# Even mixer of a hybrid trunk: the depthwise convolution shared between VectorE and TensorE by channels and token parity, with the weight splits of that stage on VectorE

## The chip, the core and the metric

The kernel runs on one core of one Trainium2 chip. The metric is the device time of one execution in microseconds. The median of three runs of the kernel before is 970.71 us (969.78 to 971.41). TensorE is the matrix engine, VectorE (DVE), ScalarE (ACT) and GpSimd (POOL) are the three engines for elementwise work, SyncE (SP) issues the weight loads.

## The reference

The program is a trunk of two layers on 256 tokens of 1024 channels, all in float32. Each layer is a gated feed-forward, a token mixer and another feed-forward, each added to the residual. The mixer of the first layer, the even one, is the stage of this case:

```python
def even_mixer(h, w_in, w_out, conv_w, conv_b, ln_g, ln_b, q_g, k_g, sinks):
    proj = h @ w_in
    a_val, a_gate, q, k, v = jnp.split(proj, cuts, axis=-1)      # 512, 512, 512, 128, 128 columns
    u = a_val * jax.nn.sigmoid(a_gate)
    u = lax.conv_general_dilated(u, ...) + conv_b                # causal, per channel, 31 taps
    u = jax.nn.silu(layer_norm(u, ln_g, ln_b))                   # over the 512 channels
    q = rms_norm(q, q_g); k = rms_norm(k, k_g)                   # per head of 64
    o, _, _ = banded_attention(q, k, v, 127, sinks)              # 8 query heads, 2 key heads
    return jnp.concatenate([u, o], axis=-1) @ w_out
```

`h` is the residual after a root-mean-square norm with a gain per channel; the factor `1/rms` of a token is applied after the product.

## The kernel before, in words

Activations lie with tokens on partitions, in two halves `t` of 128 tokens and two halves `d` of 512 channels. A product needs them transposed as the stationary operand (four 128x128 blocks through `transposed`, L238), and streams the weights. Every float32 product is carried by three passes: both operands are split exactly into `hi` and `lo` (L308), and hi·hi, lo·hi and hi·lo are summed in PSUM.

**Weights.** A plan lists units of up to 128x2048. `take` keeps four of them in flight: SyncE loads a unit into a raw buffer, ScalarE copies it to `hi`, and the difference `lo` comes from VectorE in pieces of 1024 columns or, for the units named in `on_pool` (10 of the even mixer, 5 of the odd one), from GpSimd in one piece of 2048. The four split buffers turn over as TensorE reads them.

**Order.** Outside the even mixer all engines are in a scheduler's order. In the even mixer (`even_rest`, L512 on) VectorE and TensorE follow the order in which the code is written, by `manual_schedule`; `FILL`, `O_BEFORE` and `O_MID` say how many taps or matmuls stand between which steps. A wait at one instruction of VectorE holds everything written behind it. ScalarE and GpSimd stay with the scheduler.

**The even mixer before.**
1. `even_mixer` multiplies the normed input by the first 512 columns of `w_in` (two PSUM banks `gv`): values and gates of 256 channels. GpSimd computes the factor `1/rms` (`finish`, L271 to L256), ScalarE the sigmoid `sg`, VectorE the gated `u` (L564). TensorE transposes `u`, ScalarE copies it into `uT`, whose first 30 columns are zero (L570).
2. The same for the other 256 channels; then the products for `q` and for `k` and `v`. ScalarE makes their squares, VectorE the head sums (L381), then the inverse root for all 20 heads (12 small operations, L245 to L253) and `k` and `q` times it (L389, L395).
3. The convolution has four tiles of 128 channels by 256 tokens. Tiles 0 to 2 are taps on VectorE (L548 and L552: `acc += uT[:, k:k+256] * w`), 93 in all, spread over the mixer. Tile 3 is 31 products on TensorE with diagonal matrices `diag`, built by GpSimd (L519), each float32 product as two records.
4. Attention: for each of eight heads the scores (L412, L413), masks and maxima (L417), the exponential, the transposes of the probabilities (L426) and the values (L432 to L434), with `fill(i)` putting taps and convolution products between.
5. `attention_out` normalises and transposes `o`; `mixer_first` multiplies it by its rows of `w_out`. In between the convolution's result is transposed back (`cn`, L643), VectorE takes its mean and variance (L644 on) and normalises it (`yn`, L651), TensorE transposes again (`yt`), ScalarE applies gain, bias and silu, and `mixer_last` adds the last products. `x_80` to `x_83` are the four quarters of the residual (L492), and the next norm's `xg`, `xth`, `xtl` follow.

Of the kernel before, what the change touches and what calls it, by code (L numbers as in the profile page):

```python
# [9 lines left out]

# [13 lines left out]
EPS = 1e-6  # L24
# [12 lines left out]
O_BEFORE = 13  # L37
O_MID = 22
FILL = (8, 9, 18, 21, 7, 7, 5, 8)
PE_TAPS = [(3, k) for k in range(31)]  # L40
# [3 lines left out]
def tile_trunk(ctx: ExitStack, tc: tile.TileContext, x, norm_g, w_gate, w_up, w_down,  # L44
# [108 lines left out]
    on_pool = set(range(ev0 + 5, ev0 + 15)) | set(range(od0 + 10, od0 + 15))  # L153
# [7 lines left out]
    def unit():  # L161
        """The next unit's loads, and the steps of its split."""
# [58 lines left out]
    def split_steps(src, name, gain=None, tag="st", bufs=12):  # L221
        """[128, 4, 128] values in PSUM or SBUF -> hi and lo, times a gain per partition and chunk."""
# [18 lines left out]
    def inv_sqrt(ss, scale, n, eng=nc.vector):  # L241
        """1 / sqrt(ss * scale + EPS): a first guess from the exponent's bits, then Newton's steps."""
# [47 lines left out]
    def projects(xp, cols):  # L290
        """Two banks, one per token half, with cols of x_normed @ w before rstd, and the steps to fill them."""
        ps = [bank(f"pj{t}") for t in range(2)]
        steps = []
        for kh in range(2):
            hi, lo = take()
            for t in range(2):
                h, l = xp.parts[t, kh]
                steps += products(ps[t], h, l, hi, lo, cols, FULL, kh == 0, kh == 1)
        return ps, steps
# [6 lines left out]
    def run(steps, n=None):  # L306
        for _ in range(len(steps) if n is None else min(n, len(steps))):
            steps.pop(0)()  # L308
# [66 lines left out]
    def head_sums(ps, r, heads, ss, name):  # L375
        """ps * r in SBUF, and the sums of squares of its heads of 64 columns."""
# [7 lines left out]
    def head_norm(q, rh, heads, paired=False):  # L384
        """Heads of 64 columns times their factors rh, in place or, paired, to head order (c, s)."""
# [81 lines left out]
    def mixer_first(ys, src):  # L467
        """Steps for ys = src @ the later rows of w_out."""
        steps = []
        for d in range(2):  # L470
            hi, lo = take()
            for t in range(2):
                steps += products(ys[t][d], *src[t], hi, lo, 512, FULL, True, False)
        return steps
# [37 lines left out]
    def even_rest(xp, nxt, gv):  # L512
        uT = [slot("uT") for _ in range(4)]
        for c in range(4):
            nc.gpsimd.memset(uT[c][:, 0:PAD], 0.0)
        diag = [slot("diag", "hl"[i % 2]) for i in range((len(PE_TAPS) + 3) // 4)]
        diags = [diag[i // 4][:, (i % 4) * 128:(i % 4) * 128 + 128] for i in range(len(PE_TAPS))]
# [3 lines left out]
        on_pe = {c: [(dg, k) for dg, (cc, k) in zip(diags, PE_TAPS) if cc == c] for c in range(4)}  # L521
        on_dve = {c: [k for k in range(TAPS) if (c, k) not in PE_TAPS] for c in range(4)}
        part = {c: work.tile([128, S], F32, name=f"part{c}", tag=f"part{c}", bufs=1) for c in range(4) if on_pe[c]}
        acc = [work.tile([128, S], F32, name=f"acc{c}", tag=f"acc{c}", bufs=1) if on_dve[c] else part[c]
               for c in range(4)]

        def pe_conv(c):
            steps = []
            for i, (dg, k) in enumerate(on_pe[c]):
                steps.append(partial(pe_tap, c, i, dg, k))  # L530
            return steps

        pc = {}

        def pe_tap(c, i, dg, k):
            if not pc:
                pc[0] = sbank("pc")
                pc.update({c: pc[0][:, S * j:S * (j + 1)] for j, c in enumerate(sorted(part, reverse=True))})
            nc.tensor.matmul(pc[c], dg, uT[c][:, k:k + S], start=i == 0, stop=i == len(on_pe[c]) - 1)  # L539
            if c == min(part) and i == len(on_pe[c]) - 1:  # L540
                for e in part:
                    nc.scalar.activation(part[e], pc[e], AF.Identity, bias=vo[:, e:e + 1])

        def dve_tap(c, i, k):
            w = cw[:, k * 4 + c:k * 4 + c + 1]
            src = uT[c][:, k:k + S]
            if i:
                nc.vector.scalar_tensor_tensor(acc[c], src, w, acc[c], op0=ALU.mult, op1=ALU.add)  # L548
            elif c in part:
                nc.vector.tensor_scalar(acc[c], src, w, None, op0=ALU.mult)  # L550
# [3 lines left out]
        order = [(c, i) for i in range(TAPS) for c in (0, 1)] + [(c, i) for i in range(TAPS) for c in (2, 3)]  # L554
        taps = [partial(dve_tap, c, i, on_dve[c][i]) for c, i in order if i < len(on_dve[c])]
        filler = [f for c in range(3, -1, -1) for f in pe_conv(c)]

        def gated(ps, j, t):
            """Channels 256 j .. of ps's values times its gates, transposed into uT."""
            sg, u = nat("sg"), nat("u")  # L560
            nc.scalar.activation(sg[:, :256], ps[t][:, :256], AF.Sigmoid, scale=xp.r[t])
            if j and t:
                warm(AF.Exp, sg[:, 0:1])
            nc.vector.scalar_tensor_tensor(u[:, :256], ps[t][:, 256:], xp.r[t], sg[:, :256], op0=ALU.mult, op1=ALU.mult)  # L564
            return u

        def to_uT(u, j, t):
            pt = transposed(u, 2)
            for c in range(2):
                nc.scalar.activation(uT[2 * j + c][:, PAD + t * 128:PAD + (t + 1) * 128], pt[:, c], AF.Copy)  # L570

        us = [gated(gv, 0, t) for t in range(2)]
        gv, steps = projects(xp, 512)
        for t in range(2):
            run(steps, FILL[t])
            to_uT(us[t], 0, t)
        run(steps)
        run(taps, FILL[2])
        us = [gated(gv, 1, t) for t in range(2)]
        qps, steps = projects(xp, 512)  # L580
        for t in range(2):
            run(steps, FILL[t])
            to_uT(us[t], 1, t)
        run(steps)
        hs = work.tile([128, 20], F32, name="hs", tag="hs", bufs=1)
        qns, kns = [], []
        for t in range(2):
            run(taps, FILL[3 + t])
            qns.append(head_sums(qps[t], xp.r[t], 8, hs[:, 8 * t:8 * t + 8], "q"))
        kps = project(xp, 256)  # L590
        for t in range(2):
            run(taps, FILL[5 + t])
            kns.append(head_sums(kps[t], xp.r[t], 2, hs[:, 16 + 2 * t:18 + 2 * t], "k"))
        rh = inv_sqrt(hs, 1.0 / 64, 20)
        run(filler, 16)
# [231 lines left out]
```

## Time and profile before

| | us |
|---|---|
| median of three runs | 970.71 (969.78 to 971.41) |
| span of the profiled execution | 970.1 |
| TensorE busy | 938.1 (97%) |
| VectorE busy | 544.6 (56%) |
| ScalarE busy | 449.7 (46%) |
| GpSimd busy | 144.3 (15%) |

The profile is of one execution, and its span, from the first to the last instruction, is the time of that execution that it shows. The page has the busy times of the engines, the span in 40 slices with the clock that TensorE was granted, and the chain of work that ended last. Behind it stand the trace's answers: waits by engine, timelines, groups by form, and busy times by stretch. The mixer of this case lies between about 206 and 322 us.

### The profile page before, as it was taken

What the parts mean: (1) busy time and instruction counts of PE and PEld (TensorE: products, weight loads), DVE (VectorE), ACT (ScalarE), POOL (GpSimd) and SP (SyncE); (2) the same over time, 40 slices, a digit from 0 to 9 for tenths busy, and PEclk for the clock granted to TensorE, in tenths of its full rate; (3) what the DMA queues carried; (4) which work ended last, traced back from release to release, by engine and by line L of the source; (5) the groups of instructions that cost most, each with busy time, mean ns of one, the idle gap of its engine ahead of it and who ended that gap; (6) DMA issues with size and microseconds to landing.
All of it is one profiled execution on the core that took longest, in us unless ns stands there. A gap on an engine that the chain in (4) does not pass through costs nothing.

```text
span 970.1 us, 11193 instructions
## 1 busy us (share of the span) xinstructions
PE 938.1 (97%) x4363; PEld 773.4 (80%) x4363; DVE 544.6 (56%) x720; ACT 449.7 (46%) x644; POOL 144.3 (15%) x183
## 2 busy tenths in 40 slices
PE   7999999997499899999999999999999999999998
PEld 5888887876488788888778888887788888888876
DVE  6755564469985655546556555545653275555551
ACT  5644453443253554444434444454467464444440
POOL 3000001943503300000002000000063170000000
PEclk9999999998889999999999999999999999999999
DMA  8855555635501465555556555556564066555540
GB/s 293 299 176 192 174 177 172 201 102 130 173 1 53 162 199 195 163 174 186 193 173 218 174 184 178 180 190 218 189 199 149 1 217 217 174 175 189 183 148 22
DMA packets 91973, 164.74 MB, mean 170 GB/s; under 512 B 3824, under 2 KB 17968, under 8 KB 91920
## 3 DMA queue, kind: packets, MB, share of 16 engines
q1 hardware_dynamic: 91120, 163.07, 51.3%
q0 software_dynamic: 736, 0.93, 0.3%
q8 instruction: 34, 0.56, 0.2%
q14 instruction: 19, 0.16, 0.0%
q10 hardware_dynamic: 64, 0.02, 0.0%
HBM read 162.96 MB, written 1.05 MB: 169 GB/s over the span
## 4 chain that ended last, share of the span: by engine, by line
PE 93%; DVE 6%; DMA 1%; ACT 0%; issue 0%; POOL 0%; DVEq 0%; POOLq 0%
PE pj L308 56%; PE y L201 25%; PE pt L238 3%; DVE acc L548 3%; PE m L201 2%; PE m L308 2%; PE sc L412 1%; PE pc L539 1%; PE pp L426 1%; DMA sink_b<-in_ev_sinks_dram 1%; DVE acc L552 1%; DVE xtl L308 0%; PE o L433 0%; PE o L434 0%; PE sc L413 0%; PE o L432 0%
## 5 line engine op out<-in xcount | busy, mean ns | idle before, releaser
L308 DVE TENSOR_TENSOR lo<-raw,hi 128x1024 fp32r<-128x1024 f32 (+2 forms) x286 | 333.2, 1200 | 236.8 <-ACT hi L308 230.7
L308 ACT ACTIVATE hi<-raw 128x1024 fp32r<-128x1024 f32 (+3 forms) x301 | 307.5, 1067 | 314.1 <-PE pj L308 142.8
L308 PE MATMUL pj<-hi,xtl 128*128 128x512 f32 (+2 forms) x832 | 322.4, 388 | 3.4 <-DVE xtl L308 3.4
L308 PE MATMUL pj<-hi,xth 128*128 128x512 f32 (+2 forms) x832 | 319.6, 387 | 0.4 <-ACT xth L308 0.3
L308 PE MATMUL pj<-lo,xth 128*128 128x512 f32 (+2 forms) x832 | 226.6, 389 | 0.0
L308 PEld LDWEIGHTS pj<-hi,xtl 128*128 128x128 f32 x832 | 157.3, 189 | 33.6 <-DVE xtl L308 4.5
L308 PEld LDWEIGHTS pj<-hi,xth 128*128 128x128 f32 x832 | 157.4, 189 | 31.0 <-ACT xth L308 0.8
L308 PEld LDWEIGHTS pj<-lo,xth 128*128 128x128 f32 x832 | 155.5, 189 | 28.5
L201 PE MATMUL y<-hi,hth 128*128 128x512 f32 x352 | 138.4, 393 | 0.0
L201 PE MATMUL y<-hi,htl 128*128 128x512 f32 x336 | 131.5, 391 | 0.0
L201 PE MATMUL y<-lo,hth 128*128 128x512 f32 x352 | 101.0, 397 | 0.0
L308 POOL TENSOR_TENSOR lo<-raw,hi 128x2048 fp32r<-128x2048 f32 (+1 forms) x15 | 65.9, 4406 | 103.9 <-ACT hi L308 103.9
L201 PEld LDWEIGHTS y<-lo,hth 128*128 128x128 f32 x352 | 65.4, 188 | 18.4 <-issue 5.6
L201 PEld LDWEIGHTS y<-hi,hth 128*128 128x128 f32 x352 | 66.1, 188 | 16.0 <-issue 3.0
L201 PEld LDWEIGHTS y<-hi,htl 128*128 128x128 f32 x336 | 63.1, 188 | 12.8
L548 DVE SCALAR_TENSOR_TENSOR acc<-uT,cw,acc 128x256 f32<-128x256 f32 x90 | 55.6, 663 | 0.6
L335 DVE SCALAR_TENSOR_TENSOR h<-pj,nr,sg 128x512 f32<-128x512 f32 (+1 forms) x48 | 33.3, 693 | 38.5 <-PE pj L308 38.5
L308 ACT ACTIVATE hth<-pt 128x512 fp32r<-128x512 f32 x40 | 23.9, 597 | 59.6 <-PE pt L238 59.6
L519 POOL TENSOR_SCALAR diag<-ident,cw 128x128 f32<-128x128 f32 x31 | 26.0, 857 | 148.2 <-PE y L201 148.2
L308 DVE TENSOR_TENSOR htl<-pt,hth 128x512 fp32r<-128x512 f32 x40 | 27.6, 691 | 33.0 <-ACT hth L308 33.0
L328 ACT ACTIVATE sg<-pj,nr 128x512 f32<-128x512 f32 (+1 forms) x48 | 30.4, 636 | 30.4 <-PE pj L308 25.6
L271 POOL TENSOR_TENSOR s<-ss 128x2 f32<-128x2 f32 x5 | 4.0, 801 | 231.7 <-ACT junk L266 231.7
(173 smaller groups left out, 585.1 us busy)
## 6 DMA issues: line engine op xcount, KB each, us to landing
raw<-in_ffn_w_up_dram SPq DMA_DIRECT2D x40, 1024.0 KB, 5.1
raw<-in_ffn_w_down_dram SPq DMA_DIRECT2D x40, 1024.0 KB, 4.9
raw<-in_ffn_w_gate_dram SPq DMA_DIRECT2D x38, 1024.0 KB, 5.1
raw<-in_od_w_in_dram SPq DMA_DIRECT2D x8, 1024.0 KB, 5.0
raw<-in_ev_w_in_dram SPq DMA_DIRECT2D x10, 512.0 KB, 3.9
raw<-in_od_w_out_dram SPq DMA_DIRECT2D x4, 1024.0 KB, 4.9
raw<-in_ffn_w_gate_dram SPq DMA_DIRECT2D x8, 384.0 KB, 3.4
raw<-in_ffn_w_up_dram SPq DMA_DIRECT2D x8, 384.0 KB, 4.1
```

Source lines behind the costliest of these rows:

```text
L201: f()
L238: nc.tensor.transpose(ps[:, j * 128:(j + 1) * 128], src[:, j * 128:(j + 1) * 128], ident)
L271: eng.tensor_tensor(s2, sv[:, :, 0], sv[:, :, 1], op=ALU.add)
L308: steps.pop(0)()
L328: nc.scalar.activation(s[:, :n], gs[t], AF.Silu, scale=xp.r[t])
L335: nc.vector.scalar_tensor_tensor(h[:, :n], us[t] if fg == 5 else us[t][:, :], xp.r[t], sg[t][:, :n], op0=ALU.mult, op1=ALU.mult)
L412: nc.tensor.matmul(sc[:, 0:256], qT[1][pr, cq], kk, start=True, stop=True)
L426: nc.tensor.transpose(ps[:, j * 128:(j + 1) * 128], p[i][:, j * 128:(j + 1) * 128], ident)
L519: nc.gpsimd.tensor_scalar(dg, ident, cw[:, k * 4 + c:k * 4 + c + 1], None, op0=ALU.mult)
L539: nc.tensor.matmul(pc[c], dg, uT[c][:, k:k + S], start=i == 0, stop=i == len(on_pe[c]) - 1)
L548: nc.vector.scalar_tensor_tensor(acc[c], src, w, acc[c], op0=ALU.mult, op1=ALU.add)
L552: nc.vector.tensor_scalar(acc[c], src, w, vo[:, c:c + 1], op0=ALU.mult, op1=ALU.add)
```

## The change

It does seven things, all in or for the even mixer:

- Channels 0 to 255 keep their taps on VectorE: two tiles, 62 taps. Channels 256 to 511 go to TensorE, in four groups of 64 channels. A tile `vT` holds, on 128 partitions, 64 channels of even tokens and the same 64 channels of odd tokens, in 128 columns; 16 products with a 128x128 matrix give both parities of a group, 64 products in all. The matrices `wT` are built by 16 GpSimd products of 512 columns from `eye2` and `taps2`, constants made in the first phase (18 small VectorE operations).
- For these channels the projection takes every second token as its stationary operand (`PARITY`), so that a bank holds the even tokens and the other the odd ones. Both halves of the normed input lie in one tile `xt`.
- The factor `1/rms` is put into parity order by `parities`: two transposes, two products with the unit matrix and two sums.
- The layer norm of the convolution's result runs by parity, and the silu writes the tokens back in order.
- The ten units of the even mixer leave `on_pool`; their `lo` is made by VectorE in pieces of 1024 or 512 columns, at the places of the written order where the units are taken.
- The lists of matmuls become generators; a unit is taken when its first matmul is written.
- The order of taps and products is written out anew; ScalarE's table for the exponential is no longer loaded ahead.

```diff
-    on_pool = set(range(ev0 + 5, ev0 + 15)) | set(range(od0 + 10, od0 + 15))
+    on_pool = set(range(od0 + 10, od0 + 15))
...
+        def parities(self):
+            ps = tbank("rT")
+            for t in range(2):
+                nc.tensor.transpose(ps[:, t * 128:t * 128 + 128], self.r[t].to_broadcast([128, 128]), ident)
+            rp, junk = sm("rp", 2), nat("junk")
+            for r in range(2):
+                nc.vector.tensor_tensor(junk[:, 0:128], ps[:, r:S:2], ident, op=ALU.mult)
+                nc.vector.tensor_reduce(rp[:, r:r + 1], junk[:, 0:128], axis=AX.X, op=ALU.add)
+            return rp
+    PARITY = [slice(r, S, 2) for r in range(2)]
-    def projects(xp, cols):
+    def projects(xp, cols, tokens=HALVES):
         ps = [bank(f"pj{t}") for t in range(2)]
+        def steps():
+            for kh in range(2):
+                hi, lo = take()
+                for t in range(2):
+                    h, l = (xp.xt[kh][:, i, :, tokens[t]] for i in range(2))
+                    yield from products(ps[t], h, l, hi, lo, cols, FULL, kh == 0, kh == 1)
+        return ps, steps()
...
-        for dg, (c, k) in zip(diags, PE_TAPS):
-            nc.gpsimd.tensor_scalar(dg, ident, cw[:, k * 4 + c:k * 4 + c + 1], None, op0=ALU.mult)
+        for g in range(4):
+            for h in range(4):
+                w = slot("wT", "hl"[h % 2]).rearrange("p (j c) -> p j c", c=64)
+                nc.gpsimd.tensor_tensor(w, eye2.unsqueeze(1).to_broadcast([128, 8, 64]),
+                                        taps2[:, g, 8 * h:8 * h + 8].unsqueeze(2).to_broadcast([128, 8, 64]), op=ALU.mult)
+        def pe_conv():
+            pc = sbank("pc")
+            for g in range(4):
+                for q in range(16):
+                    w = wT[4 * g + q // 4][:, 2 * (q % 4):2 * (q % 4) + 2].rearrange("p i c -> p (i c)")
+                    yield partial(nc.tensor.matmul, pc[:, g * 128:(g + 1) * 128], w,
+                                  vT[g // 2][:, g % 2, q + 1:q + 129], start=q == 0, stop=q == 15)
+            for g in range(4):
+                yield partial(nc.scalar.activation, cv[:, g], pc[:, g * 128:(g + 1) * 128], AF.Identity,
+                              bias=bias2[:, g:g + 1])
...
+        rp = xp.parities()
+        gv, steps = projects(xp, 512, PARITY)
...
+        for t in range(2):
+            gated(gv[t], rp[:, t:t + 1], u2[:, :, t])
+        qps, steps = projects(xp, 512)
+        run(steps, 12)
+        pt = transposed(u2.rearrange("p g r c -> p (g r c)"))
+        for j in range(2):
+            nc.scalar.activation(vT[j][:, :, PADB:PADB + 128], pt[:, 2 * j:2 * j + 2], AF.Copy)
...
         def fill(i):
-            run(taps, 2 if i < 8 else 1)
-            run(filler, 2 if i < 3 else 0)
+            run(taps, 3)
+            run(conv, 6 if i < 3 else 3)
...
+        for r in range(2):
+            for c in range(2):
+                nc.tensor.transpose(cps[0][:, r * 256 + c * 128:r * 256 + (c + 1) * 128], acc[c][:, PARITY[r]], ident)
+        for g in range(4):
+            nc.tensor.transpose(back[:, g], cv[:, g], ident)
+        o = attention_out(os_, ls)
-        run(steps, O_MID)
+        run(steps, 20)
...
+            run(steps, 6)
             ps = tbank("yt")
```

**GpSimd, ahead of the mixer's norm and through the mixer.** `s` to `nr` is the norm's factor; `lo` are splits.

Before:

```order
L519 TENSOR_SCALAR diag<-ident,cw 128x128 x3
L515 MEMSET uT 128x30
L519 TENSOR_SCALAR diag<-ident,cw 128x128 x16
L271 TENSOR_TENSOR s_1553<-ss 128x2
...
L256 TENSOR_TENSOR nr<-nr,na 128x2
L308 TENSOR_TENSOR lo<-raw,hi 128x2048
```

After:

```order
L543 MEMSET vT 128x2x16
L542 MEMSET uT 128x30
L548 ISA
L548 TENSOR_TENSOR wT<-eye_229,taps_231 128x512 x16
L275 TENSOR_TENSOR s_1562<-ss 128x2
...
L275 TENSOR_TENSOR s_2555<-ss 128x2
```

The tables `wT` stand where the `diag` stood, ahead of the norm's factor, and behind that factor comes at once the next phase's `s`, with no split between.

**VectorE around the head sums of `q` and `k`.** `acc` are taps.

Before:

```order
L548 SCALAR_TENSOR_TENSOR acc_1692<-uT,cw,acc_1692 128x256
L381 TENSOR_REDUCE hs<-sq 128x8
L548 SCALAR_TENSOR_TENSOR acc_1693<-uT,cw,acc_1693 128x256
...
L548 SCALAR_TENSOR_TENSOR acc_1692<-uT,cw,acc_1692 128x256
L381 TENSOR_REDUCE hs<-sq 128x2
L548 SCALAR_TENSOR_TENSOR acc_1693<-uT,cw,acc_1693 128x256
```

After:

```order
L330 TENSOR_TENSOR lo<-raw,hi 128x1024 x2
L557 SCALAR_TENSOR_TENSOR acc_1694<-uT,cw,acc_1694 128x256
...
L406 TENSOR_REDUCE hs<-sq 128x8 x2
L557 SCALAR_TENSOR_TENSOR acc_1694<-uT,cw,acc_1694 128x256
...
L330 TENSOR_TENSOR lo<-raw,hi 128x1024 x4
L557 SCALAR_TENSOR_TENSOR acc_1694<-uT,cw,acc_1694 128x256
L557 SCALAR_TENSOR_TENSOR acc_1693<-uT,cw,acc_1693 128x256
L557 SCALAR_TENSOR_TENSOR acc_1694<-uT,cw,acc_1694 128x256
L406 TENSOR_REDUCE hs<-sq 128x2 x2
```

Splits now stand between the taps and ahead of the sums that `k` needs.

**VectorE at the end of the mixer,** from the layer norm's root `nr` to the residual.

Before:

```order
L253 SCALAR_TENSOR_TENSOR nr<-na,nr 128x2
L651 TENSOR_SCALAR yn<-cn,mv,nr 128x512 x2
L308 TENSOR_TENSOR utl<-ua,uth 128x512 x2
L492 TENSOR_TENSOR x_80<-m_2287,x_80 128x512
L492 TENSOR_TENSOR x_82<-m_2289,x_82 128x512
```

After:

```order
L251 SCALAR_TENSOR_TENSOR nr<-na,nr 128x2
L330 TENSOR_TENSOR lo<-raw,hi 128x1024 x2
L673 TENSOR_SCALAR yn<-cn,mv,nr 128x256 x4
L330 TENSOR_TENSOR lo<-raw,hi 128x1024 x2
L691 TENSOR_TENSOR utl<-ua,uth 128x512 x2
L330 TENSOR_TENSOR lo<-raw,hi 128x1024 x4
L515 TENSOR_TENSOR x_80<-m_2342,x_80 128x512
```

Pairs of splits stand ahead of `yn`, of `utl` and of `x_80`.

## Rows read from the trace of the kernel before

**Rows 1.** The page's clock line (granted clock, tenths, 40 slices) and chain by engine
```profile
PEclk9999999998889999999999999999999999999999
...
PE 93%; DVE 6%; DMA 1%; ACT 0%; issue 0%; POOL 0%; DVEq 0%; POOLq 0%
```
**Rows 2.** TensorE's waits: engine, line, waited for: us in total, times, longest
```profile
PE pk L238 <- DVE k L389: 12.2, 1, 12.2
...
PE pt L238 <- DVE u L564: 5.8, 1, 5.8
...
PE pj L308 <- DVE xtl L308: 3.4, 2, 2.9
```
**Rows 3.** Busy us (count) of PE, PEld, DVE, ACT, POOL, then PEclk, DMA share, GB/s
```profile
266.10:271.53 5.43, 5.18 (x17) 3.81 (x17) 4.76 (x13) 2.00 (x4) 0.00 (x0) 0.50 0.01 5
...
271.53:293.82 22.29, 22.29 (x138) 18.79 (x138) 18.41 (x61) 13.68 (x45) 0.00 (x0) 0.99 0.00 1
```
**Rows 4.** Timeline of VectorE and GpSimd: start, us, engine, what [idle before, releaser]
```profile
239.84 17.63 DVE L548 SCALAR_TENSOR_TENSOR acc<-uT,cw,acc 128x256 f32<-128x256 f32 x7
...
242.37 14.03 POOL L308 TENSOR_TENSOR lo<-raw,hi 128x2048 fp32r<-128x2048 f32 x3 [0.47 <-ACT hi L308]
...
257.99 2.85 DVE L548 SCALAR_TENSOR_TENSOR acc<-uT,cw,acc 128x256 f32<-128x256 f32 x7
```
**Rows 5.** Groups by form, VectorE, 200 to 325: count, busy us, mean ns, idle before
```profile
L564 DVE SCALAR_TENSOR_TENSOR u<-pj,nr,sg 128x256 f32<-128x256 f32 x4 | 1.8, 478 | 5.9 <-ACT sg L561 5.9
...
L381 DVE TENSOR_REDUCE hs<-sq 128x8 f32<-128x512 f32 x2 | 1.4, 678 | 1.8 <-ACT sq L379 1.8
...
L381 DVE TENSOR_REDUCE hs<-sq 128x2 f32<-128x128 f32 x2 | 0.6, 276 | 0.0
...
L308 DVE TENSOR_TENSOR lo<-raw,hi 128x1024 fp32r<-128x1024 f32 x4 | 4.7, 1213 | 0.0
```
**Rows 6.** Timeline of VectorE at 205 and 263
```profile
205.36 1.29 DVE L308 TENSOR_TENSOR xtl<-xg,xth 128x512 fp32r<-128x512 f32 x2
...
263.24 0.18 DVE L245 TENSOR_SCALAR nv<-hs 128x20 f32<-128x20 f32 x1
```
**Rows 7.** Timeline of GpSimd, 174 to 211; last, VectorE's splits by form, 165 to 196
```profile
174.67 3.00 POOL L519 TENSOR_SCALAR diag<-ident,cw 128x128 f32<-128x128 f32 x4
...
180.19 12.98 POOL L519 TENSOR_SCALAR diag<-ident,cw 128x128 f32<-128x128 f32 x16
...
204.62 0.88 POOL L271 TENSOR_TENSOR s<-ss 128x2 f32<-128x2 f32 x1 [11.45 <-ACT junk L266]
...
210.10 0.20 POOL L256 TENSOR_TENSOR nr<-nr,na 128x2 f32<-128x2 f32 x1
...
L308 DVE TENSOR_TENSOR lo<-raw,hi 128x1024 fp32r<-128x1024 f32 x12 | 14.5, 1233 | 11.9 <-ACT hi L308 11.9
```
**Rows 8.** Chain of waits (start, us, what); the second row from TensorE's timeline
```profile
206.10 5.29 PE pj L308 x22
...
246.79 7.07 PE L539 MATMUL pc<-uT,diag 128*128 128x256 f32 x32
...
266.10 0.46 PE pk L238
...
272.67 1.06 PE pc L539 x4
...
291.65 0.87 PE pt L238 x8
...
318.25 3.53 DVE xtl L308
```
**Rows 9.** ScalarE: timeline, then a group by form; last, weight loads on the page
```profile
289.37 1.28 ACT L313 ACT_TABLE_LOAD   x1
...
L308 ACT ACTIVATE hi<-raw 128x1024 fp32r<-128x1024 f32 x6 | 6.1, 1051 | 4.8 <-issue 3.3 <-PE pj L308 1.3 <-ACT uT L570 0.3
...
L308 PEld LDWEIGHTS pj<-hi,xtl 128*128 128x128 f32 x832 | 157.3, 189 | 33.6 <-DVE xtl L308 4.5
```

More of the change, by code (lines that the diff above doesn't have):

```diff
@@ L9 @@
 from functools import partial
+from itertools import islice
 import concourse.bass as bass
@@ L36 @@
 PRIO = 400
[L37 to L40, printed above, removed]
+PADB = 16
 @with_exitstack
@@ L288, in finish @@
             self.r = rstd_of(self.ss, eng)
-    def projects(xp, cols):
-        ps = [bank(f"pj{t}") for t in range(2)]
[L293 to L299, printed above, removed]
+        def parities(self):
[7 more added lines that the diff above has]
+            return rp
+    HALVES = [slice(t * 128, t * 128 + 128) for t in range(2)]
+    PARITY = [slice(r, S, 2) for r in range(2)]
+    def projects(xp, cols, tokens=HALVES):
+        ps = [bank(f"pj{t}") for t in range(2)]
+        def steps():
[5 more added lines that the diff above has]
+        return ps, steps()
     def project(xp, cols):
@@ L306, in run @@
     def run(steps, n=None):
-        for _ in range(len(steps) if n is None else min(n, len(steps))):
-            steps.pop(0)()
+        if isinstance(steps, list):
+            for _ in range(len(steps) if n is None else min(n, len(steps))):
+                steps.pop(0)()
+        else:
+            for f in islice(steps, n):
+                f()
     def warm(func, src):
@@ L521, in even_rest @@
[L521 to L542, printed above, removed]
@@ L544, in dve_tap @@
-        def dve_tap(c, i, k):
+            nc.gpsimd.memset(vT[c][:, :, 0:PADB], 0.0)
+        wT = []
+        for g in range(4):
[3 more added lines that the diff above has]
+                                        taps2[:, g, 8 * h:8 * h + 8].unsqueeze(2).to_broadcast([128, 8, 64]), op=ALU.mult)
+                wT.append(w)
+        acc = [work.tile([128, S], F32, name=f"acc{c}", tag=f"acc{c}", bufs=1) for c in range(2)]
@@ L555, in even_rest @@
[L555 to L565, printed above, removed]
@@ new lines, in even_rest, with gated @@
+        cv = work.tile([128, 4, 128], F32, name="cv", tag="cv", bufs=1)
+        taps = [partial(dve_tap, c, k) for k in range(TAPS) for c in range(2)]
+        conv = pe_conv()
+        def gated(ps, r, dst):
+            sg = nat("sg")
+            nc.scalar.activation(sg[:, :256], ps[:, 0:256], AF.Sigmoid, scale=r)
+            v = [w.rearrange("p (g c) -> p g c", c=64) for w in (ps[:, 256:], sg[:, :256])]
+            nc.vector.scalar_tensor_tensor(dst, v[0], r, v[1], op0=ALU.mult, op1=ALU.mult)
@@ new lines, in even_rest @@
+        rp = xp.parities()
+        u = [nat("u") for t in range(2)]
+        for t in range(2):
+            gated(gv[t], xp.r[t], u[t][:, :256].rearrange("p (g c) -> p g c", c=64))
+        gv, steps = projects(xp, 512, PARITY)
+        for t in range(2):
+            run(steps, 9)
+            pt = transposed(u[t], 2)
+            for c in range(2):
+                nc.scalar.activation(uT[c][:, PAD + t * 128:PAD + (t + 1) * 128], pt[:, c], AF.Copy)
+        run(steps, 6)
+        run(taps, 6)
@@ L585, in even_rest @@
+        run(taps, 6)
         hs = work.tile([128, 20], F32, name="hs", tag="hs", bufs=1)
[L586 to L589, printed above, removed]
+        qns = [head_sums(qps[t], xp.r[t], 8, hs[:, 8 * t:8 * t + 8], "q") for t in range(2)]
+        run(taps, 4)
         kps = project(xp, 256)
-        for t in range(2):
-            run(taps, FILL[5 + t])
-            kns.append(head_sums(kps[t], xp.r[t], 2, hs[:, 16 + 2 * t:18 + 2 * t], "k"))
+        run(taps, 3)
@@ L594, in even_rest @@
+        kns = [head_sums(kps[t], xp.r[t], 2, hs[:, 16 + 2 * t:18 + 2 * t], "k") for t in range(2)]
         rh = inv_sqrt(hs, 1.0 / 64, 20)
-        run(filler, 16)
+        run(conv, 20)
         vn = []
@@ L626, in even_rest @@
         warm(AF.Silu, es[:, 0, 0:1])
-        run(filler, 3)
         nc.vector.tensor_tensor(ls, ls, es, op=ALU.add)
-        o = attention_out(os_, ls, lambda t: (run(taps, 3), run(filler, 8)))
         run(taps)
-        run(filler)
-        for c in part:
-            if on_dve[c]:
-                nc.vector.tensor_tensor(acc[c], acc[c], part[c], op=ALU.add)
+        run(conv)
+        cps = [sbank("cn") for j in range(2)]
+        for r in range(2):
+            for c in range(2):
+                nc.tensor.transpose(cps[0][:, r * 256 + c * 128:r * 256 + (c + 1) * 128], acc[c][:, PARITY[r]], ident)
@@ L765, in tile_trunk @@
     nc.vector.tensor_scalar(gq_o, vo[:, 18:19], 0.125, None, op0=ALU.mult)
+    eye2 = const.tile([128, 64], F32, name="eye2")
+    nc.vector.tensor_tensor(eye2, ident[:, 0:64], ident[:, 64:128], op=ALU.add)
+    taps2 = const.tile([128, 4, 32], F32, name="taps2")
+    bias2 = const.tile([128, 4], F32, name="bias2")
+    nc.vector.memset(taps2, 0.0)
+    for g in range(4):
+        rows, c = slice(g % 2 * 64, g % 2 * 64 + 64), 2 + g // 2
+        for r in range(2):
+            to = slice(r * 64, r * 64 + 64)
+            nc.vector.tensor_copy(taps2[to, g, 1 - r:32 - r], cw[rows].rearrange("p (k c) -> p k c", c=4)[:, :, c])
+            nc.vector.tensor_copy(bias2[to, g:g + 1], vo[rows, c:c + 1])
     phases = [(0, partial(ffn, then=AF.Sigmoid)), (1, even_mixer), (2, ffn), (3, partial(ffn, then=AF.Exp)), (4, odd_mixer),
```

102 lines of the change are left out of this document (49 added, 53 removed).

## The prediction

> **What bounds the kernel now.** I read the page first. The chain of work that ended last is 93% TensorE [rows 1], so time can only be won where TensorE stands still or runs slowly. The clock line says where the second happens: three slices near the end of the first third fall below full speed, all of them in the even mixer (206 to 327 us), and no later slice does [rows 1]. The list of TensorE's waits says where the first happens: 12.2 us in one wait of the key transposes `pk` for VectorE's `k`, 5.8 us in one wait of the transposes of `u` for VectorE's gating, 3.4 us for the low half `xtl` of the normed input [rows 2]. That is 21.4 us, and the low clock comes right behind such waits: between 266.10 and 271.53 us the granted clock is 0.50, the lower of the two levels, after the 12.2 us of standing still [rows 3].
>
> Why is VectorE late at `k`? Its order is written down: the taps of the convolution stand ahead of the gatings and of the head sums. Seven taps took 2.85 us at 257.99, that is 0.41 each, but seven others took 17.63 us from 239.84 on, 2.5 each, while GpSimd ran three weight splits in a row [rows 4]. So a tap, which reads two tiles of SBUF, stands still behind a split on GpSimd.
>
> **The change, part by part. Stage 1, from the mixer's first gating to `pk`.** Before, TensorE goes on with its last matmuls of the first product at 206.10 for 5.29 us [rows 8], to 211.4, and `pk` starts at 266.10 [rows 8]: 54.7 us, set by VectorE. The change takes the 10 splits of this stretch off GpSimd, a third of the taps off VectorE, and puts 20 splits of half that size or less into VectorE's written order, of which 12 stand ahead of `k`. VectorE's list from the first gating to `k`, from the rows:
> - two parity factors, four operations of 128 columns, each like the small head sum at 0.28 [rows 5]: 1.1
> - four gatings at 0.45 (478 ns alone, less end to end) [rows 5]: 1.8
> - 34 taps at 0.41, no longer blocked [rows 4]: 13.8
> - 8 splits of 1024 columns at 1.2 [rows 5]: 9.6
> - 4 splits of 512 columns at 0.65, half of the 1.29 of two `xtl` [rows 6]: 2.6
> - head sums, two of 8 heads at 0.6 and two of 2 at 0.28 [rows 5]: 1.8
> - the inverse root and both `k`, from 263.24 until `pk` at 266.10 [rows 6, 8]: 2.9
>
> That is 33.6. To it I add 2.3 of waits: 0.5 until the first `uT` is there, and 1.8 because the squares of `q` stand on ScalarE behind a pair of `hi` copies of 1.05 each [rows 9]. 211.4 + 35.9 = 247.3. TensorE's own work would end near 244.0: from 206.10 to 266.10 it stood still 12.2 + 5.8 and lost about 3.4 to the clock, so 38.6 are work, to which 32 records of `pc` in 7.07 [rows 8] no longer belong; 40 of 0.109 come (half the columns of the old ones: eight 128-column transposes take 0.87 [rows 8]), and 2.0 move in from before 206.10. So VectorE still sets the end, by 3.3 us, and **the gain is 266.1 - 247.3 = 18.8**.
>
> **Stage 2, from `pk` to the next phase's first matmul (321.8).** The parts:
> - `pk` to the first scores: 5.4 before [rows 3], the same after, for TensorE stood still ahead of it again.
> - Attention. TensorE is busy all of 22.29 us there [rows 3], so what is put in is paid. Before, 12 records of `pc` lie in it, 1.06 for four [rows 8]: 3.2. After, 72 records of 0.109: 7.8. That is +4.6; ScalarE's table load of 1.28 [rows 9] now stands ahead of the last `pT`, of which TensorE's last matmuls hide most: +0.2. Together +4.8.
> - Last value product to `m`: 12 old records go (2.6), eight `cn` transposes come here (0.9), the normalisation of `o` loses its cover (0.5): -1.2.
> - In the `m` stage the `cn` transposes are gone (-0.9), but two splits of 1.2 [rows 5] stand ahead of `yn` on VectorE, and TensorE runs out at `yt`: about +2.2, less 0.3 of cover. +1.0.
> - `x_80`: two splits stand ahead of it, +2.4; but `xtl`, which took 3.53 at 318.25 behind a GpSimd split [rows 8], falls back to 0.65 [rows 6], -2.8. -0.4.
>
> Stage 2 loses 4.2.
>
> **The norm boundary, around 206.** Eight matmuls of the next product that filled the wait for `xtl` move behind it (the lazy list of the projection; 8 x 0.24 = 1.9 [rows 8], with the two `rT` transposes the 2.0 above). The start at 206.10 doesn't move by that, since `xtl` sets it [rows 2, 8], but TensorE stands still longer before it, and in this kernel a low clock followed such stretches [rows 3]: 1.0 lost.
>
> **The tap tables.** Sixteen `wT` of 512 columns replace 31 `diag` on GpSimd. By the splits of 2048 columns, three in 14.03 us [rows 4], a quarter of one is 1.17, which I take, since both operations read two tensors; by the column price of `diag`, 0.81 for 128 [rows 7], it would be 3.2, and 1.17 is the lower end. They get their slots as the second half of the feed-forward's last product frees them, in pairs: from 174.67, where a slot came free before [rows 7], every 12 matmuls of 0.24 [rows 8], so until about 195. At 1.17 the last pair ends at 197.3, ahead of GpSimd's `s` at 204.62 [rows 7]. Do they stall VectorE's splits there? Beside the `diag` 12 of VectorE's splits took 1233 ns in the mean [rows 7], against 1213 without [rows 5], so `diag` cost nothing; the GpSimd products, by rows 4, do. Of what they delay only the end counts, two of 1.17 ahead of `xtl`: 2.4, between 0 (VectorE was idle 11.9 us of that stretch [rows 7]) and 4.
>
> The Trainium skill (SBUF — State Buffer, Who interferes with whom) says that a VectorE instruction with two SBUF inputs contends with any GpSimd instruction that reads SBUF, whichever starts first holding the port for the whole instruction. By that rule `diag` would already have cost VectorE its share and the tables cost nothing new, and the sum would be 2.4 lower; the trace agrees for the splits and not for `diag`.
>
> **Costed at nothing.** The product of the gates by parity takes every second token as its stationary operand, 48 weight loads. No row shows a strided load. From below it is 0: loads of 0.189 [rows 9] lie beside matmuls of 0.24 [rows 8]. Twice as long, each would stick out by 0.14, 6.7 in all, of which TensorE's 3.3 of slack ahead of VectorE take half; so 0 to 3.4, and 0 is nearer, since nothing but the step differs. The constants of the tables are 18 small VectorE operations in the first phase, where no listed wait of TensorE names VectorE's work [rows 2]; they hide behind its matmuls, and with that cover gone they would be 18 x 0.28 = 5.0. The odd mixer's order is unchanged.
>
> **The sum.** 18.8 - 4.2 - 1.0 - 2.4 = 11.2. The profiled execution spans 970.1, 0.6 under the median of 970.71; from the median: **959.5 us**. With the bounds of the tables and the waits its own range is 954 to 964.
>
> **Rivals.**
> - A, splits late. Each pair in VectorE's written order waits for its `hi` on ScalarE, which waits for a buffer. Where that is late, taps behind it wait too: four pairs by 2.1 each, less the 1.8 counted: +6.6, 966.1. For: four buffers, and order is fixed. Against: ScalarE is half idle.
> - B, the stalls vanish. If `yt`, `x_80` and the clock cost nothing (2.2 + 2.4 + 1.0 = 5.6): 953.9. For: at `yt` and `x_80` the splits may be done before the operand behind them is ready, if ScalarE makes their `hi` early. Against: ahead of them the buffers are all taken until the matmuls that use them have run.
> - C, slower: the tables. GpSimd's root `nr` at 210.10 [rows 7], which all gatings wait for, stands behind all 16 `wT`. At 3.2 each they end at 174.7 + 51.2 = 225.9, 21.3 past 204.62, and everything behind is later by that: 959.5 + 21.3 = 980.8. It decides from 1.9 each (any delay) and turns the sign at 2.6. For: `diag`'s own price per column. Against: GpSimd's 2-column operations take 0.20 [rows 7], so nothing fixed is large, and its long products are much cheaper per column. Between 1.9 and 2.6 each it gives 960 to 971.
>
> **Chances.** Forecast 0.57, A 0.17, B 0.14, C in full 0.06, its middle 0.06. A difference under 0.2% (1.9 us) can't be told from none. Faster (under 968.8): the forecast, A without its upper tail (0.15), B, and 0.04 of C's middle, 0.90; same: the tail of A and as much of C's middle, 0.04; slower: C in full, 0.06. The range reaches from a little under B over A to most of C's middle, 952 to 969; outside lie C (0.06) and the tails of A, B and the forecast (some 0.12).
>
> **What would show it.** `pk` near 247 instead of 266; taps at 0.41 throughout; no GpSimd split between 210 and 320; attention some 5 us longer; waits of TensorE at `yt` and ahead of the norm transposes behind `x_80`; one low-clock stretch instead of two in mid-mixer. Wrong would be: `wT` over 1.9 us each, or VectorE idle for `hi` in stage 1.

## The result

The changed kernel takes 959.99 us (median of 4 runs, 959.72 to 962.70) against 971.06 for the kernel before. The ratio is 0.9892 (95% interval 0.9876 to 0.9908): 9 to 12 us faster, where 959.5 was forecast and a range of 952 to 969. The same kernel, run again later, gave a median of 961.33 and a ratio of 0.9910 (0.9891 to 0.9929).

### The profile page after: what moved, and what is told of

It is laid out like the page before. It is cut to its first block, busy times and chain, and to the rows that moved or that the text cites. A ratio compares the mean times of both kernels' runs of the same rounds, so it can differ in the third digit from the quotient of the medians.

```text
span 957.9 us, 11336 instructions
## 1 busy us (share of the span) xinstructions
PE 936.5 (98%) x4431; PEld 775.5 (81%) x4431; DVE 537.0 (56%) x735; ACT 451.4 (47%) x654; POOL 100.6 (10%) x158
## 4 chain that ended last, share of the span: by engine, by line
PE 95%; DVE 3%; ACT 1%; DMA 1%; issue 0%; POOL 0%; DVEq 0%; POOLq 0%
PE pj L333 57%; PE y L199 25%; PE pt L236 3%; PE m L199 2%; PE m L333 2%; DVE lo L330 1%; PE pc L333 1%; PE sc L437 1%; DMA sink_b<-in_ev_sinks_dram 1%; PE pp L451 1%; ACT hi L330 0%; PE sc L438 0%; PE o L459 0%; PE o L458 0%; PE o L457 0%
## 5 line engine op out<-in xcount | busy, mean ns | idle before, releaser
L330 DVE TENSOR_TENSOR lo<-raw,hi 128x1024 fp32r<-128x1024 f32 (+2 forms) x306 | 358.5, 1207 | 237.6 <-ACT hi L330 231.4
L333 PE MATMUL pj<-hi,xt 128*128 128x512 f32 (+2 forms) x1664 | 411.5, 387 | 2.6 <-ACT xt L330 1.9
L333 PEld LDWEIGHTS pj<-hi,xt 128*128 128x128 f32 x1664 | 309.1, 189 | 63.0 <-ACT xt L330 2.6
L333 PE MATMUL pj<-lo,xt 128*128 128x512 f32 (+2 forms) x832 | 224.8, 386 | 0.0
L333 PEld LDWEIGHTS pj<-lo,xt 128*128 128x128 f32 x832 | 154.5, 188 | 28.1
L330 ACT ACTIVATE hth<-pt 128x512 fp32r<-128x512 f32 x40 | 23.8, 596 | 59.7 <-PE pt L236 59.7
L236 PE MATMUL pt<-ident,h 128*128 128x128 f32 x176 | 27.6, 272 | 0.0
L330 POOL TENSOR_TENSOR lo<-raw,hi 128x2048 fp32r<-128x2048 f32 x5 | 23.4, 4687 | 35.6 <-ACT hi L330 35.6
L236 PEld LDWEIGHTS pt<-ident,h 128*128 128x128 f32 x176 | 22.1, 140 | 5.4
L330 DVE TENSOR_TENSOR xg<-pt,g_n 128x512 f32<-128x512 f32 x24 | 16.5, 687 | 16.8 <-PE pt L236 16.8
L557 DVE SCALAR_TENSOR_TENSOR acc<-uT,cw,acc 128x256 f32<-128x256 f32 x60 | 25.0, 479 | 0.0
```

Source lines behind the costliest of these rows:

```text
L236: nc.tensor.transpose(ps[:, j * 128:(j + 1) * 128], src[:, j * 128:(j + 1) * 128], ident)
```

## The profile after

The profiled execution spans 957.9 us. Below are the page's busy times, its clock line and its chain by engine; the last two answer to [rows 1]:

```profile
PE 936.5 (98%) x4431; PEld 775.5 (81%) x4431; DVE 537.0 (56%) x735; ACT 451.4 (47%) x654; POOL 100.6 (10%) x158
...
PEclk9999999999999999999999999999999999999999
...
PE 95%; DVE 3%; ACT 1%; DMA 1%; issue 0%; POOL 0%; DVEq 0%; POOLq 0%
```

TensorE is as busy as before (936.5 against 938.1, with 68 more matmul records), so the gain isn't work taken from it; it stands still for 21.4 us instead of 32.0. Its waits, to be read against [rows 2]:

```profile
PE pk L236 <- DVE k L414: 2.8, 1, 2.8
PE pt L236 <- DVE x L515: 2.4, 1, 2.4
PE pj L333 <- ACT xt L330: 1.9, 2, 1.3
PE yt L681 <- DVE yn L673: 1.5, 1, 1.5
PE o L457 <- ACT pT L453: 1.3, 1, 1.3
```

The 12.2 at `pk` is 2.8, the 5.8 at `u` is gone, and three small waits are new: behind the splits at `x` and `yt`, and behind the table load at `pT`. What VectorE did in the first stage stands in its timeline (start, us, what):

```profile
212.23 0.29 DVE L302 TENSOR_TENSOR junk<-rT,ident 128x128 f32<-128x128 f32 x1 [5.00 <-PE rT L299]
...
226.31 2.85 DVE L557 SCALAR_TENSOR_TENSOR acc<-uT,cw,acc 128x256 f32<-128x256 f32 x7
...
237.16 0.69 DVE L406 TENSOR_REDUCE hs<-sq 128x8 f32<-128x512 f32 x1 [1.63 <-ACT sq L404]
...
239.35 4.62 DVE L330 TENSOR_TENSOR lo<-raw,hi 128x1024 fp32r<-128x1024 f32 x4
```

Seven taps take 2.85, as in the free stretch of [rows 4]; the four splits ahead of `k` take 4.62; and VectorE stands idle for the squares of `q` for 1.63, where 1.8 was put. The busy times by stretch, columns as in [rows 3]; the stretches are stage 1, `pk` to the first scores, attention, and the rest up to the next phase:

```profile
211.98:248.44 36.46, 33.63 (x194) 29.23 (x193) 32.03 (x73) 18.74 (x34) 0.00 (x0) 1.00 0.60 168
248.44:253.75 5.31, 4.94 (x27) 4.59 (x27) 2.98 (x9) 3.28 (x5) 0.00 (x0) 0.68 0.11 39
253.75:279.32 25.57, 24.25 (x179) 21.84 (x179) 16.13 (x59) 13.63 (x47) 0.00 (x0) 1.00 0.00 1
279.32:311.56 32.24, 28.18 (x130) 22.40 (x128) 21.23 (x41) 12.71 (x18) 0.00 (x0) 0.95 0.38 120
...
249.00:252.00 3.00, 2.68 (x13) 2.71 (x14) 2.42 (x7) 1.78 (x5) 0.00 (x0) 0.53 0.04 11
280.00:283.00 3.00, 3.00 (x13) 2.30 (x12) 1.48 (x4) 1.20 (x2) 0.00 (x0) 0.50 0.00 0
```

Stage 1 lasts 36.5 us at the full clock, against 54.7. The granted clock is at its lower level in two short places (from 249.0 and from 279.5, some 3.5 us each) instead of three, of some 7, 14 and 3.5 us.

To compare kernels whose starts differ by a few us, I use three points of each trace: A, the first residual update at the end of the first phase's last product (VectorE `x<-y`, 195.59 here); `pk`; and H, the first gated `h` of the next phase (332.55 here). Behind H every kernel of this study takes 625.3 to 626.1 us. A lies between 193.3 and 197.1, also among kernels with the same code ahead of it, so that part differs by execution; what a kernel changes is seen from A to H.

| kernel | A to `pk` | `pk` to H | A to H |
|---|---|---|---|
| before | 71.5 | 78.3 | 149.8 |
| after | 52.9 | 84.1 | 137.0 |

## Experiments

**Two halves of the change alone.** `b_dve` is the kernel before with only the splits moved from GpSimd to VectorE; `a_pool` is the kernel after with them moved back.

```diff
-    on_pool = set(range(ev0 + 5, ev0 + 15)) | set(range(od0 + 10, od0 + 15))
+    on_pool = set(range(od0 + 10, od0 + 15))
```

(`a_pool` has the same edit the other way round, on the kernel after.) Expected of `b_dve`:

> The kernel before with one edit: the ten even-mixer units leave GpSimd, their splits go into VectorE's written order. Theory P (most of the gain is that taps no longer stand still behind GpSimd's splits): VectorE's list to k becomes 58 taps of 0.41, 12 splits, 6.5 of the rest and some 2 of waits, 44.5 us in place of 54.7, so pk near 256 and 961 to 964 us in all. Theory T (most of the gain is the 31 taps that left VectorE): the splits cost VectorE what the blocking cost, pk stays near 264, 968 to 972 us.

Expected of `a_pool`:

> The kernel after with the ten units back on GpSimd, all else as after. Theory P: the taps are blocked again, pk at 255 or later, 965 to 970 us. Theory T: VectorE has 12 fewer splits for the blocked taps, pk stays near 248, the stalls at yt (1.5) and x_80 (2.4) go and the 2.9 of a blocked xt comes back: 957 to 962 us.

Measured: `b_dve` 969.27, ratio 0.9977 (0.9965 to 0.9989); `a_pool` 967.51, ratio 0.9964 (0.9948 to 0.9980).

| kernel | A to `pk` | `pk` to H | A to H |
|---|---|---|---|
| `b_dve` | 61.7 | 85.2 | 146.9 |
| `a_pool` | 60.3 | 83.9 | 144.2 |

At `pk`, theory P's numbers are met or nearly met and T's are missed: `pk` is at 255.5 in `b_dve` (P put 256, T 264) and at 254.6 in `a_pool` (P put 255 or later, T 248). But neither half carries most of the gain there: alone they win 9.8 and 11.2, together 18.6. The whole time of `a_pool` is in P's range and that of `b_dve` in T's, for each half alone pays nearly the whole loss behind `pk` (6.9 and 5.6), for reasons of its own, and both together pay 5.8. `b_dve` waits 4.9 at `yt`, since pairs of splits stand between its last taps and `yn`, and TensorE's clock is at its lower level behind that wait, from 295.5 to 302.9; TensorE's waits there:

```profile
PE pk L238 <- DVE k L389: 9.3, 1, 9.3
...
PE yt L657 <- DVE yn L651: 5.1, 2, 4.9
PE pt L238 <- DVE x L492: 2.4, 1, 2.4
```

`a_pool` pays the convolution in attention and still has 2.9 at the blocked `xt`. Its taps ahead of `k` show the blocking again (timeline of VectorE and GpSimd):

```profile
229.68 19.75 POOL L330 TENSOR_TENSOR lo<-raw,hi 128x2048 fp32r<-128x2048 f32 x4 [3.66 <-ACT hi L330]
236.30 15.00 DVE L557 SCALAR_TENSOR_TENSOR acc<-uT,cw,acc 128x256 f32<-128x256 f32 x7
```

Seven taps in 15.00 us, blocked as in the kernel before (17.63 [rows 4]). So ahead of `pk` the two wins nearly add up and behind it the loss is paid once: the change is worth 11 and its halves 2 and 4. The half that `b_dve` leaves out holds the taps that left VectorE and all the rest of the change, its order and its lists; no run takes these apart.

**The tables doubled.** `a_wt2` writes each `wT` twice.

```diff
-                nc.gpsimd.tensor_tensor(w, eye2..., taps2..., op=ALU.mult)
+                for _ in range(2):
+                    nc.gpsimd.tensor_tensor(w, eye2..., taps2..., op=ALU.mult)
```

> The kernel after with each of the 16 tables wT written twice by GpSimd. If GpSimd's order binds (the slower rival C): 32 tables of 1.53 end near 223 instead of 198.6, nr and all behind it come 18 us later, 975 to 980 us. If the tables are off the path: 959 to 962 us. If only VectorE's splits beside them suffer: 961 to 966 us, with nr in its place and TensorE waiting for lo before 206.

Measured: 974.11, ratio 1.0035 (1.0024 to 1.0046), slower than the kernel before and 0.9 under the range that was put for C. GpSimd's timeline after, then of `a_wt2`, and TensorE's wait in `a_wt2`:

```profile
174.02 24.54 POOL L548 TENSOR_TENSOR wT<-eye,taps 128x512 f32<-128x512 f32 x16 [1.68 <-PE y L199]
205.22 0.87 POOL L275 TENSOR_TENSOR s<-ss 128x2 f32<-128x2 f32 x1 [6.66 <-ACT junk L270]
```

```profile
171.70 45.40 POOL L549 TENSOR_TENSOR wT<-eye,taps 128x512 f32<-128x512 f32 x32 [1.68 <-PE y L199]
217.06 0.20 POOL L275 TENSOR_TENSOR s<-ss 128x2 f32<-128x2 f32 x1
```

```profile
PE rT L299 <- POOL nr L254: 7.8, 1, 7.8
```

The 32 tables take 1.42 each in the mean (45.40 / 32), the 16 of the kernel after 1.53, for not all of them lie beside VectorE's splits. With 16 GpSimd idles 6.66 ahead of `s`; with 32 `s` comes 14.2 later against the start of the tables (45.36 against 31.20), where 18 was expected from 1.53 each, and A to H is 14.4 longer (151.4). The mechanism of rival C is real, one to one; only its price isn't reached.

**The wait ahead of the norm, and where a split is written.** `a_hoist` writes nine matmuls of the second product ahead of the parity factors, to fill TensorE's wait near 204. `a_hoist2` is the same, with the splits that the earlier `take` prepares written where they were.

```diff
+        gv1 = gv
+        gv, steps = projects(xp, 512, PARITY)
+        run(steps, 9)
         rp = xp.parities()
...
-        gv, steps = projects(xp, 512, PARITY)
-        for t in range(2):
-            run(steps, 9)
...
+        for t in range(2):
+            run(steps, 9 * t)
```

> The kernel after with the first nine matmuls of the second product (by parity) written ahead of the parity factors, so that they can fill TensorE's wait for the normed input near 204. If VectorE's list from nr to k sets pk: nr at 210.7 lets it start 1.0 earlier at most, 958.5 to 959.5 us. If TensorE's time there is worth all it takes: 2.0 less, 957.5 to 958.3 us. If the weights for it are late: no change.

> As a_hoist, but the splits of the unit that the earlier take prepares stay where the kernel after has them, behind the gatings; only TensorE's order differs from the kernel after. Theory S (a_hoist lost because a pair of splits came ahead of the parity factors and the sigmoids): TensorE's idle time near 204 is used and the factors start when nr is there, 958 to 959.5 us. Theory M (the matmuls themselves are in the wrong place): 962 to 964 us, as a_hoist.

Measured: `a_hoist` 963.54 (0.9923, 0.9908 to 0.9938), against every expectation; `a_hoist2` 959.54 (0.9884, 0.9864 to 0.9904), no different from after. In `a_hoist` VectorE's timeline shows why:

```profile
213.00 2.36 DVE L330 TENSOR_TENSOR lo<-raw,hi 128x1024 fp32r<-128x1024 f32 x2 [5.02 <-ACT hi L330]
215.28 0.28 DVE L302 TENSOR_TENSOR junk<-rT,ident 128x128 f32<-128x128 f32 x1
```

The pair of splits came ahead of the parity factors, in the very list that sets `pk`; TensorE then waited 4.1 for `u`. Theory S holds as to the cause: with the splits back in their place the loss is gone. But the factors don't start earlier in `a_hoist2`, as S had it: they start 16.6 behind A, as in the kernel after, since the first product with the low half of `xt` comes 11.1 behind A in both and the transposes `rT` stand behind it. The nine matmuls fill the wait near 204 and are missing behind `rT`: TensorE waits 2.1 for `u` there, its clock is at the lower level from 212.5 to 216.5, and `pk` keeps its 2.8. Time won on TensorE ahead of VectorE's list is handed back.

**The small waits.** `a_tail` writes one pair of splits behind `yn` and one behind the residual adds; `a_kdefer` writes the four splits ahead of the head sums of `k` behind `k` and `q`. Both let `take` put a unit's split steps into a list that is run later.

```diff
-    def take():
-        prepare(cursor[0] + WB)
+    def take(late=None):
+        prepare(cursor[0] + WB, late)
...
+        run(late)
```

> The kernel after with two pairs of splits written later: one behind yn, one behind the residual adds x_80 and x_82. If these splits held VectorE at the end of the mixer: the waits at yt (1.5) and x_80 (2.4) go, 955.5 to 957.5 us. If the later splits then hold the next phase's norm or its weights: 959 to 961 us, with a new wait behind x_80.

> The kernel after with the four splits between the taps and the head sums of k written behind k and q. If VectorE's list sets pk: the wait of 2.8 at pk falls to 1 or less, 957 to 958.5 us. If the splits then stand ahead of the masks in attention: that is given back, 959.5 to 961 us.

`a_all` has both, `a_hoist2` and a later load of the silu table:

> The three edits together, and the load of the silu table written behind the normalised o, so that it doesn't stand ahead of the last pT (1.3). If the waits add up: 951 to 954.5 us. If they hide each other or the clock falls anew: 955 to 958 us.

Measured: `a_tail` 961.13 (0.9901, 0.9876 to 0.9926), `a_kdefer` 962.20 (0.9903, 0.9869 to 0.9937) and `a_all` 959.39 (0.9891, 0.9860 to 0.9921): nothing gained, and all three lie above the highest time that was put for them. In `a_tail` the waits at `yt` and `x_80` are gone as expected, and `pk` to H is 83.3, 0.8 shorter; the rest is held by TensorE's waits for `xt`, which grow from 1.9 and 0.5 to 3.7 and 1.4, and by a low clock in four places, where the two executions of the kernel after have two and three. In `a_kdefer` the wait at `pk` is 0.6, A to `pk` 50.7; but the four splits now stand ahead of the masks, TensorE waits 1.9 at the scores, the clock is low from 256.5 to 263.5, and `pk` to H grows to 88.1. There the second expectation was right in kind, not in size. In `a_all` the waits for `u` (2.1), at the scores (1.9) and for `xt` are there again, and the silu table and `cv` still stood ahead of the last `pT`, for ScalarE's order is the scheduler's.

**What does stay gained.** `a_conv` fills the wait at `pk` from the other side: 32 instead of 20 convolution products ahead of `pk`, and three instead of six behind each of the first heads.

```diff
-        run(conv, 20)
+        run(conv, 32)
...
-            run(conv, 6 if i < 3 else 3)
+            run(conv, 3)
```

> The kernel after with 32 instead of 20 of the convolution's products written ahead of pk and three instead of six after each of the first heads. If TensorE's wait of 2.8 at pk is really free time: attention is 12 products of 0.23, 2.7 us, shorter, 956.5 to 958 us. If pk is held by TensorE's own order instead: pk comes later by as much, 959.5 to 961 us.

`a_best` is `a_tail` with two of `a_kdefer`'s four splits behind `k` and `q` and two behind the first head's masks, and the silu table's load tied to the transposed `o`; the seven taps that stood in these two places move behind the last head. `after_again` is the kernel after beside them. `a_best2` is `a_conv` with `a_tail` and that load.

> The kernel after, unchanged, beside the next two: 959 to 961.5 us.

> The late splits of a_tail; the four splits ahead of k's head sums put behind k, two of them behind the first head's masks; the silu table loaded behind the transposed o. If the waits at pk (2.2 of 2.8), yt (1.5), x_80 (2.4) and pT (1.2) go and stay gone: 952.5 to 955.5 us. If the clock of TensorE falls as often as in a_tail: 955.5 to 958.5 us.

> The convolution's order of a_conv, the late splits of a_tail and the late silu table together; the splits ahead of k's head sums stay. If what a_conv won and the waits at yt (1.5) and x_80 (2.4) add up: 951 to 953.5 us. If TensorE's clock takes it back as in a_tail: 954.5 to 957 us.

| kernel | us | ratio to before | A to `pk` | `pk` to H |
|---|---|---|---|---|
| `after_again` | 961.33 | 0.9910 (0.9891 to 0.9929) | 54.0 | 84.1 |
| `a_conv` | 956.44 | 0.9860 (0.9844 to 0.9876) | 54.0 | 79.5 |
| `a_best` | 955.38 | 0.9850 (0.9835 to 0.9865) | 51.8 | 79.0 |
| `a_best2` | 954.55 | 0.9839 (0.9820 to 0.9859) | 52.9 | 78.0 |

`a_conv` gains 4.6 behind `pk`, more than the 2.7 of its products: TensorE no longer stands still ahead of `pk`, and the clock stays high at `pk` and behind attention, where it falls in both executions of the kernel after. `a_conv`, `a_best` and `a_best2` beat the kernels before and after; their intervals overlap, so they aren't told apart. For `a_best2` the sum of the waits, 951 to 953.5, was too hopeful by one us or more. Its time is in the other range, but not by the clock, which falls in one place only (304 to 308): the waits at `yt` and `x_80` are gone, and in their place TensorE's longest waits in the mixer and at the norms are for the copies of `xt`.

```profile
PE pj L337 <- ACT xt L334: 3.7, 3, 1.7
PE pj L337 <- DVE xt L334: 1.5, 2, 1.0
```

## Why the prediction was right, term by term

| term | forecast | measured |
|---|---|---|
| stage 1 | +18.8 | +18.2 (54.7 to 36.5) |
| tables and clock around 206 | -3.4 | +0.1 |
| attention | -4.8 | -6.8 (18.8 to 25.6) |
| last value product to `m` | +1.2 | +0.6 (3.5 to 2.9) |
| `m` to the transposes of `x_80` | -3.4 | -4.0 (22.6 to 26.5) |
| `x_80` to H | +2.8 | +4.2 (28.0 to 23.8) |
| sum, with +0.1 from `pk` to the scores | +11.2 | +12.4 |

(The -1.0 and -0.4 of the forecast are shown as -3.4 up to `x_80` and +2.8 behind it. The profiled execution after runs 0.6 to 0.7 late through its first phase, so at H the two traces are 11.9 apart; the medians of all runs are 11.1 apart.)

- **Stage 1** came out operation by operation: taps at 0.41, splits at 1.16 to 1.18, and the wait for the squares at 1.63. It is the term that carries the sum. Its two parts erred against each other: the list took some 32.5 instead of 33.6, and the waits 3.7 instead of 2.3, for besides the squares and the first `uT` (0.56) VectorE waits 1.04 for a `hi` and 0.4 for sigmoids. That VectorE, and not TensorE, sets `pk` was forecast with 3.3 of slack; the wait at `pk` is 2.8.
- **The tables** were put at 1.17 each and take 1.53. The price itself was near: in `a_wt2`, once VectorE has nothing left beside them, a table takes 1.04. What was left out is that VectorE's splits slow the tables too, up to 2.02 (durations in ns, least, median and most):

```profile
L548 POOL TENSOR_TENSOR wT<-eye,taps x16: 1038/1613/2022, 174.0 to 196.5; 128x512 f32<-128x512 f32 x16
```

  And the tables hold up VectorE's splits, as forecast and as the timeline after shows:

```profile
183.26 3.44 DVE L330 TENSOR_TENSOR lo<-raw,hi 128x1024 fp32r<-128x1024 f32 x2 [3.53 <-ACT hi L330]
188.71 3.98 DVE L330 TENSOR_TENSOR lo<-raw,hi 128x1024 fp32r<-128x1024 f32 x2 [2.00 <-ACT hi L330]
194.10 1.57 DVE L330 TENSOR_TENSOR lo<-raw,hi 128x1024 fp32r<-128x1024 f32 x1 [1.42 <-ACT hi L330]
```

  A pair that takes 2.35 alone took 3.44 and 3.98. But VectorE had 1.4 to 3.5 of idle time ahead of each, so the step that failed is "two of 1.17 ahead of `xtl`": the tables were done at 198.6, and nothing of theirs was left when `xt` was due (first product behind it at 206.69, 206.10 before, in an execution that ran 0.6 to 0.7 late). The lower bound, 0, was the right end.

  The prediction read "`diag` cost nothing" from VectorE's splits alone (1233 ns beside it, 1213 without [rows 5, 7]). The contention was there, on GpSimd's side; `diag` in the kernel before:

```profile
L519 POOL TENSOR_SCALAR diag<-ident,cw x31: 598/605/2464, 167.0 to 192.6; 128x128 f32<-128x128 f32 x31
```

  A `diag` takes 0.60, but the three that meet a pair of splits take 2.39 to 2.46, so the 0.81 of rival C's price has such waits in it. The Trainium skill (SBUF — State Buffer, Who interferes with whom) says that a VectorE instruction with two SBUF inputs contends with a GpSimd instruction that reads SBUF, and the traces agree for both operations: beside the tables both engines pay, beside `diag` nearly all is paid by GpSimd. (Where the prediction says that by this rule the sum would be 2.4 lower, it is the time that would be; the gain would be 13.6.)
- **The clock** at the boundary, 1.0, comes and goes between executions. In the profile after, TensorE kept its full clock behind a stretch of 3.4 us with only two matmuls, up to 206.69; in `after_again`, with the same instructions and a like stretch up to 207.27, it did not. First after, then `after_again` (columns as above):

```profile
207.00:210.00 3.00, 3.00 (x14) 2.44 (x13) 0.24 (x1) 0.00 (x0) 2.26 (x11) 1.00 0.59 175
```

```profile
203.00:206.00 3.00, 1.34 (x7) 0.70 (x5) 2.35 (x3) 3.00 (x6) 0.21 (x1) 1.00 0.46 159
206.50:209.50 3.00, 2.82 (x6) 1.90 (x7) 1.32 (x3) 0.00 (x0) 2.37 (x9) 0.50 0.54 150
```

  A to `pk` is 1.1 longer there (54.0 against 52.9), the 1.0 of the forecast. In mid-mixer the forecast had one low stretch where there are two: the one from 279.5, behind the wait at the last `pT`, costs up to 1.8 (3.5 us at half the clock, an estimate) in the two rows that meet at `m`, each of which came out 0.6 worse than forecast.
- **Attention** was too cheap by 2.0. The 72 convolution records took 8.7, not 7.8: 0.12 to 0.13 each, where the price of 0.109 came from transposes. And the table load's 1.28 with the copies `cv` was not hidden (+0.2 forecast): TensorE waits 1.3 at the last `pT`, having run out of products. ScalarE's timeline after:

```profile
275.48 1.28 ACT L338 ACT_TABLE_LOAD   x1
276.77 0.20 ACT L338 ACTIVATE warm<-es 128x1 f32<-128x1 f32 x1
276.88 1.12 ACT L333 ACTIVATE cv<-pc,bias 128x128 f32<-128x128 f32 x4
277.88 0.51 ACT L453 ACTIVATE pT<-pp 128x384 f32<-128x384 f32 x1
```
- **The stalls** at `yt` and `x_80` were forecast at 2.2 and 2.4 and are 1.5 and 2.4. Behind `x_80` the gain is 1.4 larger than forecast: the blocked `xtl` cost 2.9 [rows 8], and the low clock behind it went too. In the kernel before, the stretch of 5 us there was granted 0.66, which is 1.7 lost:

```profile
322.00:327.00 5.00, 5.00 (x18) 4.01 (x19) 4.87 (x7) 1.24 (x3) 0.00 (x0) 0.66 0.76 227
```

- **Costed at nothing.** Where the stationary operand takes every second token, TensorE needs 2.80 for twelve matmuls instead of 2.72, some 0.3 in all, well inside its slack ahead of `pk`. The 18 constants show nothing: A lies between 193.3 and 197.1 in the kernels that make them, and at 193.8 and 194.6 in the two that don't.
- **The rivals.** A didn't happen: VectorE waits for a `hi` in stage 1 once, 1.04; that is one of the prediction's two signs of being wrong, but too short to matter. Of B only the clock at the boundary came, and in one execution of two. C is real and was 0.4 us per table away (1.53 each, a delay from 1.9).

So the range held, and the time lies within 0.5 us of the forecast, but that closeness is partly luck: the boundary was 3.5 too dear, attention 2.0 too cheap, the other terms together 0.3 too cheap, and the profiled execution's gain is 0.8 larger than the medians'.

## What to carry to other kernels

Find the engine whose written list sets the end of a stage and add up that list; what is moved off it counts until the engine that waits runs out of slack (18.2 of stage 1 here; in `a_kdefer` 4.6 of splits moved off brought `pk` 2.2 forward), and what is won on the engine that waits counts nothing until the list is shorter (`a_hoist2`). Then look for what the moved work stands ahead of in its new place: `a_kdefer` gave its gain back in attention. Where an order is written by hand, the place of a `take` is the place of a split: moving a product forward can drag a split ahead of the work that everyone waits for (`a_hoist`). A wait that remains can be filled with work of the engine that waits (`a_conv`, 4.6 us behind `pk` with its clock); moving VectorE's splits about paid as much only when all of them found a free place (`a_best`).

## What the runs showed of the chip

Beside GpSimd operations on two SBUF tensors of 2048 columns, VectorE's taps took 2.1 to 2.5 each instead of 0.41. Beside such operations of 512 columns a pair of splits took 3.44 and 3.98 instead of 2.35, and the GpSimd operations up to 2.02 instead of 1.04: both engines pay. Beside GpSimd operations on a single tensor of 128 columns and a scalar per partition the splits took 1233 ns instead of 1213, while the GpSimd operation stood for up to 2.46 instead of 0.60: there GpSimd pays nearly alone. Taking every second token as the stationary operand made a weight load 193 ns instead of 188. The same kernel on the same inputs kept or lost the higher clock of TensorE behind a stretch of 3.4 us with two matmuls, which made 1.1 us from A to `pk`; a difference of that size between two traces can be the clock's alone.
